# The skip path of a hybrid encoder layer moved into the attention stage, and the first softmax map left unscaled

## The chip, the cores and the metric

One NeuronCore of a Trainium2 chip runs the kernel. The metric is the device time of one execution in microseconds, the median of several runs. TensorE, VectorE (DVE), ScalarE (ACT), GpSimd (POOL) and SyncE (SP) each work through a queue of their own in order; transfers are issued by the queue of an engine and carried out by 16 DMA engines.

## What is computed

One encoder layer on x of 1024 tokens by 1024 channels, float32. x is normalised row by row (LayerNorm with ln_emb). One input projection of width 6688 feeds two groups that run side by side: a bidirectional state-space group (convolution, chunked scan in both directions, gated RMS norm) and a differential attention of 8 heads. Both outputs, 2 x 1024 channels, go through one output projection, and the result is added to the skip path and normalised. What matters for the change:

```
h = layer_norm(x, ln_emb_g, ln_emb_b)
probs = softmax(scores, axis=-1)
w = probs[:, :, 0] - lam * probs[:, :, 1]
o = einsum("bhqs,bshe->bqhe", w, v)
o = rms_norm(o, subln_g) * (1.0 - lam_init)
y_attn = o * silu(g)
mix = einsum("bse,ed->bsd", concat([y_ssm, y_attn]), w_out)
out = layer_norm(ALPHA * h + mix, ln_g, ln_b)
```

`rms_norm` divides by the square root of the mean square plus 1e-5. If a query's row of w is multiplied by the sum s0 of its first map's exponentials, o grows by s0, and the RMS norm gives the same result when 1e-5 is replaced by 1e-5 times s0 squared. That is what lets the first map stay unscaled.

## The kernel before

**Stages.** The kernel normalises x, transposes it and keeps it in SBUF as a high and a low part (`hh`, `hl`), so that three fast matmuls stand for one float32 product. The input projection runs as 52 blocks of 128 output channels (`fill`, L328), each with 48 matmuls of 128x512. Weights are loaded by SP (`wst`), their high part is cast by ScalarE (`whi`) and the low part subtracted by GpSimd (`wlo`). The state-space group uses TensorE up to about 430 us, the attention from there. The output projection (`project_out`, L1245) has 16 units of 48 matmuls: for each of 8 token blocks `tb` a part 0 (the state-space half) and a part 1 (the attention half). Part 0 can run while head 7 is still at work; part 1 needs all heads. The rows of w_out are cast and split as they come (`rows_out`, L1137: tiles `ws`, `oh`, `ol`, later `or`).

**What sets the order.** The work is written as lanes (Python generators), and a planner, `Loom` (L46), chooses which lane goes on next, from ranks and margins in `LANES` (L29) and from costs that it assumes for each operation (L175 to L213). TensorE's order is what the planner chose; the other engines' instructions are put in order by the framework's own scheduler from its estimates, and then each engine runs its queue strictly in that order. SP issues every transfer of this kernel (`dma`, L250). All engine calls go through one helper, so nearly all rows carry its line, L140; tiles tell them apart.

**Attention of one head.** `scores` (L981): for each of 8 query blocks two score maps of 128x1024 in PSUM (`sc`), VectorE subtracts the distance penalty and takes the row maximum (`p`, `nm`), ScalarE takes the exponential with its row sum `ls`. `combine` (L1016): VectorE takes reciprocals of both sums (`rs`), multiplies one by the negative lambda, GpSimd multiplies the first map by its reciprocal (L1028; in head 7 ScalarE does, L1026), and VectorE combines both maps. `values` (L1033): TensorE transposes the combined map, ScalarE and VectorE evict it as a high and a low part (`wh`, `wl`), and it is multiplied with v. `finish` (L1070), once for each half head of 512 queries: squares (`osq`, `osh`, `osl`), their sum over channels by TensorE, the RMS factor (`msq`, `rt`) and the gate; four stores to `yd` in DRAM. PSUM banks for all but the scores come from a ring of four (`bk`).

**Skip path.** `residuals` (L1189) starts when the memory of head 6 is given back, near 1000 us. For each token block and half row it loads x (`xr`, L1212), computes `nmr` on VectorE, normalises on ScalarE, multiplies by ALPHA times the gain (`g_e`) and adds ALPHA times the bias (`b_e`) on GpSimd. `project_out` adds the PSUM result of part 0 to `xr` on VectorE (L1280) and `norm_out` (L1221) does the last LayerNorm with `g_o`, `b_o`. Pieces of the token blocks 5 to 7 are loaded late, into tiles that the attention gives back.

**Other transfers that the change touches.** `z_block` (L466) stores SiLU(z) to DRAM (`zd<-zs`, 16 of 256 KB, L478). `proj_k` (L909) copies each half of the key tile to the other partitions (`kk<-kk`, 32 of 128 KB, L921).

Of the kernel before, what the change touches and what calls it, by code (L numbers as in the profile page):

```python
# [27 lines left out]

LANES = dict(weights=(0, 0.8), channels=(1, 1.2), steps=(2, 1.6), z_tail=(2, 0.8), conv=(3, 1), v_tail=(3, 0.4), states=(4.4, 0.8), diag=(4.125, 0.6), maps=(4.4, 0.6), gate=(4.375, 0.2), finish=(4.2, 2), scores=(4, 0.8), combine=(4.125, 0.6), values=(4.25, 0.4), fill=(9, 0.8), rows_out=(9, 0.2), y_out=(9, 3), residuals=(9, 2), project_out=(9, 2))  # L29

# [186 lines left out]
def hybrid_layer_kernel(  # L217
# [14 lines left out]
    AO = Engine(loom, nc.scalar, "ACT", _act_cost, pinned=True)  # L232
    SP = Engine(loom, nc.sync, "DMA", _dma_cost)
    x, out = x[0], out[0]
    w_in, w_out, conv_w = w_in[0], w_out[0], conv_w[0]
# [14 lines left out]
    def dma(dst, src):  # L250
        SP.dma_start(dst, src)

    def transpose(dst, src, n=128):
# [111 lines left out]
    acs_dr = [dr.tile([16, NCH, 128], F32, name=f"acs_d{d}") for d in range(2)]  # L365
    zd = [dr.tile([NCH, 128, 512], F32, name=f"zd{g}") for g in range(2)]


# [97 lines left out]
    def z_block(g, j, when=None):  # L466
        def evac(half, ps):
            zr = late["sq"].tile([128, 512], F32, name="zr", bufs=2)
            A.copy(zr, ps)

            def tail():
                pt = bank((128, 4, 128))
                yield (zr, pt)
                for i in range(4):
                    transpose(pt[:, i, :], zr[:, 128 * i:128 * i + 128])
                zs = late["sq"].tile([128, 4, 128], F32, name="zs", tag="zr", bufs=2)
                A.activation(zs, pt, AF.Silu)
                dma(zd[g][4 * half:4 * half + 4, :, 128 * j:128 * j + 128].rearrange("c p n -> p c n"), zs)  # L478
                G[g].z_done += 1
            loom.add(tail(), "z_tail")  # L480
        queue.append(Block(Z0 + 512 * g + 128 * j, evac, when))
# [397 lines left out]
    class Head:  # L879
        def __init__(self, h):  # L880
            self.pool = lambda: ep if h % 2 == 0 else att["op"]
            self.q, self.k, self.v, self.g = [], 0, 0, 0
            self.scored = self.summed = self.done = 0

# [24 lines left out]
    def proj_k(h):  # L909
        H = heads_[h]  # L910

        def evac(half, ps):
            if half == 0:
                H.kk = H.pool().tile([128, 2, S], F32R, name="kk")
                H.kl = H.pool().tile([128, S], F32R, name="kl")
            t = slice(512 * half, 512 * half + 512)
            for m in range(2):
                a, b = slice(64 * m, 64 * m + 64), slice(64 - 64 * m, 128 - 64 * m)
                A.copy(H.kk[a, m, t], ps[a])
                V.tensor_sub(H.kl[a, t], ps[a], H.kk[a, m, t].bitcast(F32))  # L920
                dma(H.kk[b, m, t].bitcast(F32), H.kk[a, m, t].bitcast(F32))  # L921
            H.k += 1
        queue.append(Block(K0 + 128 * h, evac, free_since(h, "scored", 8)))
# [57 lines left out]
    def scores():  # L981

        for h, H in enumerate(heads_):
            m_h = 2.0 ** -(h + 1)
            for tb in range(8):
                yield lambda: len(H.q) > tb // 4 and H.k == 2
                yield lambda: count["s"] - count["t"] < 2
                nm = ap.tile([128, 2], F32, name="nm", bufs=2)
                ls = ap.tile([128, 2], F32, name="ls", bufs=2)
                q = H.q[tb // 4]  # L990
# [12 lines left out]
                for m in range(2):  # L1003
# [5 lines left out]
                    A.activation(p, p, AF.Exp, scale=-1.0, bias=nm[:, m:m + 1],  # L1009
                                 accum_out=ls[:, m:m + 1])  # L1010
                    pm_.append(p)
# [4 lines left out]
    def combine():  # L1016

        for _ in range(64):
            yield lambda: bool(raw_maps)
            H, tb, (p0, p1), ls = raw_maps.pop(0)  # L1020
            yield (p1, ls)
            rs = ap.tile([128, 2], F32, name="rs", bufs=2)
            V.reciprocal(rs, ls)
            V.tensor_mul(rs[:, 1:2], rs[:, 1:2], neg_lam)
            if H is heads_[7]:
                A.activation(p0, p0, AF.Copy, scale=rs[:, 0:1])  # L1026
            else:
                P.tensor_scalar(p0, p0, rs[:, 0:1], 1.0, op0=ALU.mult, op1=ALU.mult)  # L1028
            yield p0
            V.scalar_tensor_tensor(p0, p1, rs[:, 1:2], p0, op0=ALU.mult, op1=ALU.add)  # L1030
            maps_.append((H, tb, p0))

    def values():  # L1033
# [36 lines left out]
    def finish(H, o, half):  # L1070

        h = heads_.index(H)
        osq = ap.tile([128, 512], F32, name="osq")
        A.activation(osq, o, AF.Square)
# [28 lines left out]
    queue[-2].pair = queue[-1].last = True  # L1103
    for lane in (scores, combine, values):
        loom.add(lane())
# [78 lines left out]

    res = {}
    used = set()
    halves = [slice(0, 512), slice(512, 1024)]

    def residuals():  # L1189

        yield lambda: "pool" in res
        for n, src in (("g", ln_emb_g), ("b", ln_emb_b)):
            res[n] = res["pool"].tile([128, D], F32, name=n + "_e")
            dma(res[n], src.partition_broadcast(128))
            A.activation(res[n], res[n], AF.Copy, scale=ALPHA)
        late = [("zr", 2), ("zr", 2), ("o", 2), ("o", 2), ("osq", 1), ("msq", 1)]
        for tb in range(8):
# [5 lines left out]
            xr = []  # L1203
            nmr = ap.tile([128, 1], F32, name="nmr", bufs=2)
            V.scalar_tensor_tensor(nmr, mv[tb][:, 0:1], -1.0, rstd[tb], op0=ALU.mult, op1=ALU.mult)
# [11 lines left out]
        for n, src in (("g", ln_g[0]), ("b", ln_b[0])):  # L1217
            res[n + "o"] = res["pool"].tile([128, D], F32, name=n + "_o", tag=n + "_e")
            dma(res[n + "o"], src.partition_broadcast(128))

# [97 lines left out]
```

## Time and profile before

| | |
|---|---|
| median of 3 runs | 1236.02 us (1235.99 to 1239.23) |
| the profiled execution's own time | 1237.79 us |
| its span | 1236.1 us |
| mean granted TensorE clock, share of full speed | 0.989 |
| instructions | 16491 |

The profile is of one execution. Busy time counts an engine's instructions, not its waits. A wait is put down to the event that came last before the instruction could start. "Granted clock" is TensorE's, as a share of 2.4 GHz; its lower level is 1.2 GHz.

### The profile page before, as it was taken

The numbers are of one execution on the slowest core, as the hardware profiler recorded it, in microseconds if no ns is written. First come the engines' busy times: TensorE is split into PE (matmuls) and PEld (weight loads), VectorE is DVE, ScalarE is ACT, GpSimd is POOL, SyncE is SP. The second block draws the span as 40 slices with busy tenths as digits, with TensorE's granted clock in tenths as the row PEclk, the third lists the DMA queues.
The fourth block names the chain that finished last, engine by engine and source line by source line (L and its number), as shares of the span: only waits on it lengthen the run. The fifth ranks groups of instructions, "written<-read, shape, count | busy, mean of one in ns | idle before, by whom it ended". The sixth has DMA issues, their size and how long they took to land. (4 is left out here: it accounts for less than half of the span.)

```text
span 1236.1 us, 16491 instructions
## 1 busy us (share of the span) xinstructions
PE 1177.5 (95%) x5881; PEld 923.5 (75%) x5881; DVE 903.5 (73%) x1303; ACT 702.8 (57%) x1281; POOL 472.6 (38%) x404
## 2 busy tenths in 40 slices
PE   5999999899989999999999999999999998999997
PEld 3777667788667777778787777878778776778885
DVE  6686876767875568788788887887878889952334
ACT  4557478734468456565655657556655686641221
POOL 7412564322753223323232333233232429541354
PEclk9999999999999999999999999999999999989999
DMA  6113236522345521011111121121111262233221
GB/s 198 34 32 116 81 110 173 181 65 53 99 118 149 151 63 43 26 46 50 26 48 39 43 53 26 34 52 36 43 36 42 86 225 83 74 103 114 77 86 60
DMA packets 107592, 98.04 MB, mean 79 GB/s; under 512 B 9364, under 2 KB 79349, under 8 KB 107509
## 3 DMA queue, kind: packets, MB, share of 16 engines
q1 hardware_dynamic: 107509, 96.98, 27.4%
q8 instruction: 46, 0.75, 0.3%
q14 instruction: 37, 0.30, 0.1%
HBM read 75.85 MB, written 16.91 MB: 75 GB/s over the span
## 5 line engine op out<-in xcount | busy, mean ns | idle before, releaser
L140 PE MATMUL bk<-hh,whi 128*128 128x512 f32 x832 | 353.8, 425 | 1.3 <-DVE yt L140 0.7
L140 PE MATMUL bk<-hl,whi 128*128 128x512 f32 x832 | 328.1, 394 | 3.3 <-POOL hl L140 3.0
L140 PE MATMUL bk<-hh,wlo 128*128 128x512 f32 x832 | 328.9, 395 | 0.0
L140 POOL TENSOR_TENSOR wlo<-wst,whi 128x512 fp32r<-128x512 f32 x104 | 160.4, 1546 | 145.1 <-ACT whi L140 129.0
L140 ACT ACTIVATE p<-p,nm 128x1024 f32<-128x1024 f32 x128 | 146.8, 1148 | 121.3 <-DVE nm L140 120.6
L140 POOL TENSOR_SCALAR p<-p,rs 128x1024 f32<-128x1024 f32 x56 | 64.5, 1152 | 350.1 <-DVE rs L140 300.4
L140 PEld LDWEIGHTS bk<-hh,whi 128*128 128x128 f32 x832 | 158.3, 190 | 33.8 <-issue 5.7
L140 PEld LDWEIGHTS bk<-hh,wlo 128*128 128x128 f32 x832 | 157.2, 189 | 35.3
L140 PEld LDWEIGHTS bk<-hl,whi 128*128 128x128 f32 x832 | 158.3, 190 | 33.2 <-POOL hl L140 5.5
L140 DVE CUSTOM_DVE_ANT_0 p<-sc,dist 128x1024 f32<-128x1024 f32 x128 | 151.3, 1217 | 11.9 <-PE sc L140 11.2
L140 DVE SCALAR_TENSOR_TENSOR p<-p,rs,p 128x1024 f32<-128x1024 f32 x64 | 127.8, 1997 | 22.6 <-POOL p L140 18.0
L140 DVE TENSOR_TENSOR wl<-bk,wh 128x512 fp32r<-128x512 f32 x128 | 86.9, 683 | 16.1 <-ACT wh L140 14.2
L140 ACT CAST wh<-bk 128x512 fp32r<-128x512 f32 x128 | 74.1, 579 | 43.1 <-PE bk L140 42.4
L140 ACT CAST whi<-wst 128x512 fp32r<-128x512 f32 x104 | 64.0, 621 | 44.4 <-PE bk L140 37.5
L140 PE MATMUL bk<-ident,p 128*128 128x128 f32 x512 | 79.9, 279 | 4.7 <-DVE wl L140 3.0
L140 PEld LDWEIGHTS bk<-ident,p 128*128 128x128 f32 x512 | 61.9, 142 | 29.5 <-DVE wl L140 6.5
L140 ACT ACT_TABLE_LOAD x46 | 59.0, 1283 | 27.9 <-DVE t L140 17.2
L140 PE MATMUL bk<-wh,vh 128*128 128x256 f32 x256 | 74.6, 291 | 0.0
L140 PE MATMUL bk<-wl,vh 128*128 128x256 f32 x256 | 72.2, 282 | 0.9 <-DVE wl L140 0.9
L140 PE MATMUL sc<-kk,q 128*128 128x512 f32 x256 | 72.4, 394 | 0.0
L140 PE MATMUL bk<-wh,vl 128*128 128x256 f32 x256 | 72.0, 281 | 0.0
L140 PEld LDWEIGHTS bk<-xt,t 128*128 128x128 f32 x256 | 44.9, 189 | 24.3 <-issue 15.8
(217 smaller groups left out, 2168.3 us busy)
## 6 DMA issues: line engine op xcount, KB each, us to landing
wst<-in_w_in_dram SPq DMA_DIRECT2D x104, 256.0 KB, 3.0
t<-acs_d SPq DMA_DIRECT2D x64, 256.0 KB, 3.4
ws<-in_w_out_dram SPq DMA_DIRECT2D x32, 256.0 KB, 3.1
ys<-yd SPq DMA_DIRECT2D x32, 256.0 KB, 3.1
xb<-in_x_dram SPq DMA_DIRECT2D x8, 512.0 KB, 6.3
zd<-zs SPq DMA_DIRECT2D x16, 256.0 KB, 3.0
gz<-zd SPq DMA_DIRECT2D x16, 256.0 KB, 3.1
yd<-ys SPq DMA_DIRECT2D x16, 256.0 KB, 2.5
```

Source lines behind the costliest of these rows:

```text
L140: r = f(*args, **kw)
```

## The change

1. The skip path is computed in a new lane, `skip_rows`, during the attention: 16 pieces of 128x512, one after every third query block, each loaded, normalised (ScalarE), multiplied and added to (GpSimd) and stored to DRAM (`xr_dram`). `residuals` only loads the finished pieces. `g_o` and `b_o` are loaded before head 7.
2. The first map is not scaled. The second map's factor becomes -lam times s0 / s1, with one map-wide operation in `combine` instead of two. Every four query blocks ScalarE squares s0 with the factor sqrt(1e-5) (`e2`) and sends the 512 values through DRAM (`ed`); `finish` loads them as a row over all partitions (`er`) and adds them where 1e-5 was added.
3. The RMS factor's refinement takes one VectorE operation less.
4. ScalarE's queue issues the stores of zs, the copies of kk and those of ed.
5. The memory set aside for another kind of DMA is cut to 1024 bytes, which makes room for the new tiles.

The new lane has rank 9, margin 2. The diff, cut:

```diff
+    AD = Engine(loom, nc.scalar, "DMA", _dma_cost)
+    def dma_act(dst, src):
+        AD.dma_start(dst, src)
+    xr_dram = [dr.tile([128, D], F32, name=f"xrd{b}") for b in range(NCH)]
-                dma(zd[g][4 * half:4 * half + 4, :, 128 * j:128 * j + 128].rearrange("c p n -> p c n"), zs)
+                dma_act(zd[g][4 * half:4 * half + 4, :, 128 * j:128 * j + 128].rearrange("c p n -> p c n"), zs)
-                dma(H.kk[b, m, t].bitcast(F32), H.kk[a, m, t].bitcast(F32))
+                dma_act(H.kk[b, m, t].bitcast(F32), H.kk[a, m, t].bitcast(F32))
-                ls = ap.tile([128, 2], F32, name="ls", bufs=2)
+                if tb % 4 == 0:
+                    ls = ap.tile([128, 4, 2], F32, name="ls", bufs=2)
 ...
-            rs = ap.tile([128, 2], F32, name="rs", bufs=2)
-            V.reciprocal(rs, ls)
-            V.tensor_mul(rs[:, 1:2], rs[:, 1:2], neg_lam)
-            if H is heads_[7]:
-                A.activation(p0, p0, AF.Copy, scale=rs[:, 0:1])
-            else:
-                P.tensor_scalar(p0, p0, rs[:, 0:1], 1.0, op0=ALU.mult, op1=ALU.mult)
-            yield p0
-            V.scalar_tensor_tensor(p0, p1, rs[:, 1:2], p0, op0=ALU.mult, op1=ALU.add)
+            rs = ap.tile([128, 1], F32, name="rs", bufs=2)
+            V.reciprocal(rs, ls[:, tb % 4, 1:2])
+            V.scalar_tensor_tensor(rs, rs, ls[:, tb % 4, 0:1], neg_lam, op0=ALU.mult, op1=ALU.mult)
+            V.scalar_tensor_tensor(p0, p1, rs, p0, op0=ALU.mult, op1=ALU.add)
             maps_.append((H, tb, p0))
+            if tb % 4 == 3:
+                e2 = ap.tile([128, 4], F32, name="e2", bufs=2)
+                A.activation(e2, ls[:, :, 0], AF.Square, scale=math.sqrt(EPS))
+                ed = dr.tile([4, 128], F32, name="ed", bufs=2)
+                    dma_act(ed.rearrange("t p -> p t"), e2)
+                H.ed.append(ed)
 ...
+        er = ap.tile([128, 512], F32, name="er")
+        dma(er, H.ed[half].rearrange("t p -> (t p)").partition_broadcast(128))
-        V.tensor_scalar(ms, pms, 1.0 / 128, EPS, op0=ALU.mult, op1=ALU.add)
+        V.scalar_tensor_tensor(ms, pms, 1.0 / 128, er, op0=ALU.mult, op1=ALU.add)
 ...
-        V.tensor_mul(ms, ms, rt)
-        V.tensor_scalar(ms, ms, -0.5, 1.5, op0=ALU.mult, op1=ALU.add)
+        V.scalar_tensor_tensor(ms, ms, -0.5, rt, op0=ALU.mult, op1=ALU.mult)
+        V.scalar_tensor_tensor(rt, ms, 1.5, rt, op0=ALU.add, op1=ALU.mult)
-        V.tensor_mul(rt, rt, ms)
 ...
+    def skip_rows():
+        for n, src in (("g", ln_emb_g), ("b", ln_emb_b)):
+            resid[n] = ap.tile([128, D], F32, name=n + "_e")
+            dma(resid[n], src.partition_broadcast(128))
+        yield lambda: count["s"] > 1
+        for n in "gb":
+            A.activation(resid[n], resid[n], AF.Copy, scale=ALPHA)
+        left = []
+        def store():
+            dst, t = left.pop(0)
+            dma(dst, t)
+        for i in range(16):
+            tb, t = i // 2, slice(512 * (i % 2), 512 * (i % 2) + 512)
+            yield lambda: count["s"] >= 3 * i + 3
+            if len(left) > 1:
+                store()
+            xe = ap.tile([128, 512], F32, name="xe", bufs=2)
+            dma(xe, x[128 * tb:128 * tb + 128, t])
+            nmr = ap.tile([128, 1], F32, name="nmr", bufs=2)
+            V.scalar_tensor_tensor(nmr, mv[tb][:, 0:1], -1.0, rstd[tb], op0=ALU.mult, op1=ALU.mult)
+            A.activation(xe, xe, AF.Identity, scale=rstd[tb], bias=nmr)
+            P.tensor_mul(xe, xe, resid["g"][:, t])
+            P.tensor_add(xe, xe, resid["b"][:, t])
+            left.append((xr_dram[tb][:, t], xe))
+        yield lambda: count["s"] >= 54
+        while left:
+            store()
+        for n, src in (("g", ln_g[0]), ("b", ln_b[0])):
+            res[n + "o"] = ap.tile([128, D], F32, name=n + "_o", tag=n + "_e")
+            dma(res[n + "o"], src.partition_broadcast(128))
 ...
-                dma(xr[n], x[128 * tb:128 * tb + 128, t])
-                A.activation(xr[n], xr[n], AF.Identity, scale=rstd[tb], bias=nmr)
-                P.tensor_mul(xr[n], xr[n], res["g"][:, t])
-                P.tensor_add(xr[n], xr[n], res["b"][:, t])
+                dma(xr[n], xr_dram[tb][:, t])
 ...
```

`count["s"]` is the number of query blocks whose scores are done, 64 in all.

## Rows read from the trace of the kernel before

**Rows 1.** The page's first part: busy time, share of the span, instructions, by engine.

```profile
PE 1177.5 (95%) x5881; PEld 923.5 (75%) x5881; DVE 903.5 (73%) x1303; ACT 702.8 (57%) x1281; POOL 472.6 (38%) x404
```

**Rows 2.** Busy time by stretch: length, PE, PEld, DVE, ACT, POOL, granted clock, DMA share, GB/s.

```profile
430.00:980.00 550.00, 548.11 (x2943) 432.70 (x2941) 440.90 (x659) 334.19 (x581) 168.59 (x124) 1.00 0.17 43
980.00:1100.00 120.00, 108.67 (x553) 85.98 (x552) 98.42 (x139) 83.34 (x138) 59.95 (x41) 0.96 0.39 123
1100.00:1228.30 128.30, 128.28 (x554) 103.76 (x552) 48.43 (x83) 28.93 (x45) 55.54 (x45) 1.00 0.28 88
```

**Rows 3.** TensorE's timeline from 975 to 1100: start, us, work, [idle before, releaser].

```profile
1021.41 0.39 PE L140 MATMUL bk<-wl,vh 128*128 128x256 f32 x1 [0.91 <-DVE wl L140]
...
1029.96 0.51 PE L140 MATMUL bk<-oh,oyh 128*128 128x512 f32 x1 [3.98 <-DVE xr L140]
...
1047.76 1.09 PE L140 MATMUL bk<-oh,oyh 128*128 128x512 f32 x2 [1.02 <-DVE wl L140]
...
1086.29 1.11 PE L140 MATMUL bk<-ident,p 128*128 128x128 f32 x4 [2.87 <-DVE wl L140]
```

**Rows 4.** Busy time by stretch, columns as in rows 2, after the two long gaps.

```profile
1029.96:1034.65 4.69, 4.69 (x15) 3.77 (x16) 4.66 (x6) 4.69 (x9) 4.69 (x4) 0.64 0.18 59
...
1086.29:1092.78 6.49, 6.49 (x20) 5.34 (x21) 4.41 (x7) 2.31 (x4) 1.72 (x2) 0.54 0.37 105
```

**Rows 5.** The chain that ended last, around the gap at 1083: start, us, what.

```profile
1078.59 4.24 DMA xr<-in_x_dram
...
1082.93 0.04 ACT xr L140
...
1083.65 0.61 ACT or L140
...
1085.63 0.61 DVE wl L140
```

**Rows 6.** Groups of VectorE from 1016 to 1062: count, busy us, mean ns, idle before.

```profile
L140 DVE TENSOR_TENSOR oyl<-ys,oyh 128x512 fp32r<-128x512 f32 x5 | 8.1, 1636 | 0.0
L140 DVE SCALAR_TENSOR_TENSOR p<-p,rs,p 128x1024 f32<-128x1024 f32 x4 | 7.4, 1862 | 0.7 <-ACT p L140 0.6
...
L140 DVE SCALAR_TENSOR_TENSOR nmr<-mv,rstd 128x1 f32<-128x1 f32 x6 | 5.3, 889 | 1.2 <-ACT xr L140 1.1
```

**Rows 7.** VectorE's timeline, the same two operations with GpSimd idle.

```profile
995.39 1.28 DVE L140 SCALAR_TENSOR_TENSOR p<-p,rs,p 128x1024 f32<-128x1024 f32 x1 [0.36 <-ACT p L140]
...
1008.76 0.68 DVE L140 TENSOR_TENSOR oyl<-ys,oyh 128x512 fp32r<-128x512 f32 x1
```

**Rows 8.** Busy time of the tile xr alone: length, DVE, ACT, POOL, clock, DMA.

```profile
980.00:1100.00 120.00, 5.34 (x8) 10.03 (x13) 39.36 (x26) 0.96 0.39 123
```

**Rows 9.** Groups from 430 to 1000, columns as in rows 6.

```profile
L140 DVE SCALAR_TENSOR_TENSOR p<-p,rs,p 128x1024 f32<-128x1024 f32 x57 | 115.6, 2028 | 18.4 <-POOL p L140 18.0 <-ACT p L140 0.4
...
L140 POOL TENSOR_SCALAR p<-p,rs 128x1024 f32<-128x1024 f32 x56 | 64.5, 1152 | 350.1 <-DVE rs L140 300.4 <-PE bk L140 49.7
```

**Rows 10.** Issues on SP by tile: count, ns least/median/most, first and last start.

```profile
L140 SPq DMA_DIRECT2D zd<-zs x16: 359/370/508, 122.2 to 392.2; - x16
...
L140 SPq DMA_DIRECT2D kk<-kk x32: 461/467/1127, 409.6 to 967.7; - x32
```

**Rows 11.** Waits: who for whom, us in total, times, longest.

```profile
ACT xr L140 <- DMA xr<-in_x_dram: 7.6, 3, 5.8
...
PE bk L140 <- DVE t L140: 3.5, 4, 1.3
...
SPq L140 <- ACT kk L140: 62.4, 16, 7.9
...
SPq L140 <- ACT zs L140: 27.8, 10, 7.2
```

**Rows 12.** Transfers: count, KB each, median us from issue to landing.

```profile
zd<-zs SPq DMA_DIRECT2D x16, 256.0 KB, 3.0
...
xr<-in_x_dram SPq DMA_DIRECT2D x16, 256.0 KB, 5.4
```

More of the change, by code (lines that the diff above doesn't have):

```diff
@@ L27 @@
 ALPHA = 2.0 ** 0.25
-LANES = dict(weights=(0, 0.8), channels=(1, 1.2), steps=(2, 1.6), z_tail=(2, 0.8), conv=(3, 1), v_tail=(3, 0.4), states=(4.4, 0.8), diag=(4.125, 0.6), maps=(4.4, 0.6), gate=(4.375, 0.2), finish=(4.2, 2), scores=(4, 0.8), combine=(4.125, 0.6), values=(4.25, 0.4), fill=(9, 0.8), rows_out=(9, 0.2), y_out=(9, 3), residuals=(9, 2), project_out=(9, 2))
+LANES = dict(weights=(0, 0.8), channels=(1, 1.2), steps=(2, 1.6), z_tail=(2, 0.8), conv=(3, 1), v_tail=(3, 0.4), states=(4.4, 0.8), diag=(4.125, 0.6), maps=(4.4, 0.6), gate=(4.375, 0.2), finish=(4.2, 2), skip_rows=(9, 2), scores=(4, 0.8), combine=(4.125, 0.6), values=(4.25, 0.4), fill=(9, 0.8), rows_out=(9, 0.2), y_out=(9, 3), residuals=(9, 2), project_out=(9, 2))
 def col_bcast(ap, n):
@@ L882, in __init__ @@
             self.q, self.k, self.v, self.g = [], 0, 0, 0
+            self.ed = []
             self.scored = self.summed = self.done = 0
@@ L1009, in scores @@
                     A.activation(p, p, AF.Exp, scale=-1.0, bias=nm[:, m:m + 1],
-                                 accum_out=ls[:, m:m + 1])
+                                 accum_out=ls[:, tb % 4, m:m + 1])
                     pm_.append(p)
@@ L1021, in combine @@
             yield (p1, ls)
-            rs = ap.tile([128, 2], F32, name="rs", bufs=2)
-            V.reciprocal(rs, ls)
-            V.tensor_mul(rs[:, 1:2], rs[:, 1:2], neg_lam)
-            if H is heads_[7]:
-                A.activation(p0, p0, AF.Copy, scale=rs[:, 0:1])
-            else:
-                P.tensor_scalar(p0, p0, rs[:, 0:1], 1.0, op0=ALU.mult, op1=ALU.mult)
-            yield p0
-            V.scalar_tensor_tensor(p0, p1, rs[:, 1:2], p0, op0=ALU.mult, op1=ALU.add)
-            maps_.append((H, tb, p0))
+            rs = ap.tile([128, 1], F32, name="rs", bufs=2)
+            V.reciprocal(rs, ls[:, tb % 4, 1:2])
+            V.scalar_tensor_tensor(rs, rs, ls[:, tb % 4, 0:1], neg_lam, op0=ALU.mult, op1=ALU.mult)
+            V.scalar_tensor_tensor(p0, p1, rs, p0, op0=ALU.mult, op1=ALU.add)
+            maps_.append((H, tb, p0))
+            if tb % 4 == 3:
+                e2 = ap.tile([128, 4], F32, name="e2", bufs=2)
+                A.activation(e2, ls[:, :, 0], AF.Square, scale=math.sqrt(EPS))
+                ed = dr.tile([4, 128], F32, name="ed", bufs=2)
+                with nc.allow_non_contiguous_dma(reason="512 words"):
+                    dma_act(ed.rearrange("t p -> p t"), e2)
+                H.ed.append(ed)
     def values():
@@ L1103, in hybrid_layer_kernel @@
     queue[-2].pair = queue[-1].last = True
-    for lane in (scores, combine, values):
+    resid = {}
+    def skip_rows():
[28 more added lines that the diff above has]
+            dma(res[n + "o"], src.partition_broadcast(128))
+    res = {}
+    for lane in (scores, combine, values, skip_rows):
         loom.add(lane())
@@ L1183, in y_out @@
             ahead[tb, part] = parts
-    res = {}
     used = set()
@@ L1191, in residuals @@
         yield lambda: "pool" in res
[L1192 to L1195, printed above, removed]
         late = [("zr", 2), ("zr", 2), ("o", 2), ("o", 2), ("osq", 1), ("msq", 1)]
@@ L1203, in residuals @@
             xr = []
-            nmr = ap.tile([128, 1], F32, name="nmr", bufs=2)
-            V.scalar_tensor_tensor(nmr, mv[tb][:, 0:1], -1.0, rstd[tb], op0=ALU.mult, op1=ALU.mult)
             for n, t in enumerate(halves):
@@ L1211, in residuals @@
                     xr.append(ap.tile([128, 512], F32, name="xr", tag=tag, bufs=bufs))
-                dma(xr[n], x[128 * tb:128 * tb + 128, t])
-                A.activation(xr[n], xr[n], AF.Identity, scale=rstd[tb], bias=nmr)
-                P.tensor_mul(xr[n], xr[n], res["g"][:, t])
-                P.tensor_add(xr[n], xr[n], res["b"][:, t])
+                dma(xr[n], xr_dram[tb][:, t])
             res[tb] = xr
-        for n, src in (("g", ln_g[0]), ("b", ln_b[0])):
-            res[n + "o"] = res["pool"].tile([128, D], F32, name=n + "_o", tag=n + "_e")
-            dma(res[n + "o"], src.partition_broadcast(128))
     def norm_out(tb, xr, po, final):
@@ L1304 @@
     from concourse.bass_utils import run_bass_kernel_spmd as _run
-    nc = _bacc.Bacc("TRN2", target_bir_lowering=False, num_devices=1)
+    nc = _bacc.Bacc("TRN2", target_bir_lowering=False, num_devices=1,
+                     dynamic_dma_scratch_size=1024)
     arrays, args = {}, []
```

## The prediction

> **What bounds the kernel now.** I read the page's busy shares first [rows 1]: TensorE is busy 95% of the span, VectorE 73%, ScalarE 57%. An average hides stages with different limits, so next came busy time by stretch [rows 2]. The reader should see three stages there. From 430 to 980 us, heads 0 to 6, TensorE is busy 548.11 of 550 us: whatever VectorE, ScalarE or GpSimd save there is worth almost nothing. From 980 to 1100, where head 7 runs beside the output projection, 11.3 of 120 us are idle. From 1100 to 1228.3 TensorE is full again. So the change is priced in the middle stage, and in 430 to 980 only for harm.
>
> The waits of TensorE's own timeline [rows 3] give the idle time: 0.91, 3.98, 1.02 and 2.87 us, together 8.8 us (the other 2.5 us are shorter waits, left alone here). After the two long ones the granted clock falls [rows 4]: mean 0.64 over 4.69 us and 0.54 over 6.49 us, towards 1.2 GHz from 2.4. Work lost: 0.36 x 4.69 = 1.7 us and 0.46 x 6.49 = 3.0 us. Gaps and their aftermath cost **13.5 us**; the row of 1100 to 1228.3 has no such loss.
>
> **Why those gaps exist.** The chain of waits names the path through the last of them [rows 5]: an xr load took 4.24 us, ScalarE stood until it landed, its next w_out cast and evictions came after, VectorE's subtraction after those, and TensorE lacked a free PSUM bank. The 3.98 us gap ends on VectorE's addition of xr to the product: the bank was held until the skip path was ready. Both are the in-line skip computation. VectorE is also slowed while GpSimd works: between 1016 and 1062 us, 5 oyl subtractions took 1.636 us each, 4 combinations of p 1.862 and 6 one-column nmr products 0.889 [rows 6]. Outside, an oyl took 0.68 and a combination 1.28 [rows 7]. Excess: 5 x 0.96 + 4 x 0.58 + 5.3 for nmr, which leaves this stage whole, = 12.4 us in a stretch of 46. GpSimd spends 39.36 us on xr's 26 products and sums in this stage, ScalarE 10.03 us on 13 normalisations [rows 8].
>
> **The change part by part.**
> *Skip path moved.* The stage loses those 39.36 us of GpSimd, 10.03 of ScalarE, the nmr products, and the scaling of g_e and b_e; an xr is now a plain load from DRAM, which only VectorE's addition waits for. Two parameter loads leave SP's queue here too. The 3.98 us gap goes with its slow clock: 5.7 us. The 2.87 us gap goes with its own, 5.9 us; next late there is the split of w_out, for which I leave 0.5. The 1.02 us gap stands behind VectorE's backlog and goes. The 0.91 us gap follows two ol subtractions of GpSimd that stay: I count half, 0.45. **Gain 5.7 + 5.4 + 1.0 + 0.45 = 12.5 us.** The three late pieces of xr after 1100 us lie under full TensorE: nothing.
>
> *First map unscaled.* In heads 0 to 6, 56 GpSimd products of 1.152 us (64.5 us) go [rows 9], and the combination starts that much sooner; in head 7 ScalarE did the scaling and is relieved. The cover in 430 to 980 is TensorE's own queue, so 0; head 7's share is inside the gaps above. The shorter RMS chain (one 128x512 VectorE operation fewer in each of 16 finishes) is covered the same way: 0. If the cover went, VectorE would be next, busy 441 of 550 [rows 2].
>
> *What that stage receives.* Sixteen pieces of skip path: a load, a normalisation (10.03 / 13 = 0.77 us on ScalarE), two GpSimd operations (39.36 / 26 = 1.51 us) and a store each. GpSimd thus gets 48 us back for 64.5. The issue on SP: xe has two buffers, and a load waits until the store two pieces earlier has landed, 3.0 us for such a store; the load itself took 5.4 at its median in the crowded stage [rows 12]. On SP the weight, er and y transfers queue behind that wait; TensorE waits for none of them within a few us. ScalarE's normalisation waits for the load, and the attention's exponentials and evictions queue behind it. Bounds for TensorE: below 0; above 16 x 5.8 us, the longest wait of ScalarE for an xr load [rows 11], 93 us. I take what such loads did before, 7.6 us of waiting in all over 16 loads [rows 11], of which TensorE pays a fifth: **1.5 us**. The low end is nearer because of [rows 9]: 57 combinations took 2.028 us instead of 1.28, 43 us of delay, and TensorE paid at most 1.9 us of idle time in the stage.
>
> *Issues moved from SP to ScalarE.* An issue took 0.370 us for zs and 0.467 for kk [rows 10]. In the attention 32 of kk and 16 of ed come to 48 x 0.467 = 22 us on ScalarE, busy 334 of 550. Each also waits for ScalarE's own result, with the next eviction behind it. Bounds: 0 to 22 us; I take **0.5**, by the same tolerance. SP stood 62.4 us for kk and 27.8 for zs [rows 11], but nothing of TensorE's was late behind it in the attention, so the relief there is 0. In the earlier stage the t loads stand behind zs, and TensorE waited 3.5 us for DVE t [rows 11]; the 16 zs issues cost ScalarE 5.9 us. So between a gain of 3.5 and a loss of 5.9: 0.
>
> *Epsilon row.* Sixteen squares of 128x4 on ScalarE, each between 0 and the 0.77 us of a 128x512; 512 words stored per half head, no row for that shape. Its latency is hidden behind the transposes and values of that half, and er's load behind the square and the sum over partitions; if it landed late, only head 7's last y would be late, and the other half of the output projection is there to run before it. 0.
>
> **Sum.** 12.5 - 1.5 - 0.5 = 10.5 us. The profiled execution took 1237.79 us for a span of 1236.1, and stands 1.77 over the median of 1236.02. 1236.02 - 10.5 = **1225.5 us**.
>
> **A rule that speaks against it.** VectorE operations on two SBUF tensors stretch while GpSimd runs: 1.636 us against 0.68 [rows 6, 7]. The Trainium skill, "Advanced Engine Details and Errata", section Miscellaneous Facts, GPSIMD Details, says that the Pool engine shares a read and a write interface with VectorE and conflicts with operations that have two SBUF inputs. By that rule, with which these rows agree, the stretch is not removed but moved into the attention. As a mechanism: 32 moved GpSimd operations x 0.96 us = 31 us more on VectorE. The sum holds that at 0, since GpSimd loses more than it gets; the rival below takes the other side.
>
> **The rivals.**
> *Something else fills the gaps.* The w_out splits and head 7's own chain are late by themselves, so only the 5.7 us around the xr addition is won: 1236.0 - 5.7 + 2 = 1232.3. For it: GpSimd's ol and ScalarE's or casts stand in the same chain [rows 5]. Against: each was queued behind xr work.
> *The stretch moves along.* TensorE pays a quarter of the 31 us: 1225.5 + 7.8 = 1233.3. Against: the 43 us of delay that cost it nothing.
> *ScalarE stands in line: slower.* If the normalisations reach ScalarE before their loads land, each stops every exponential and eviction. With 7.6 / 3 = 2.5 us for each of 16 pieces, 40 us, of which TensorE pays half: 1236.0 - 12.5 + 0.5 + 20 = 1244. It decides from (12.5 - 0.5) / 16 = 0.75 us of TensorE time per piece. For it: the 5.8 us wait. Against: 13 of 16 such loads caused no wait, and DMA is at 0.17 in this stage against 0.39 [rows 2].
> *More is won.* The 3.5 us behind t in the earlier stage and the 2.5 us of shorter waits go as well: 1225.5 - 6.0, about 1220.
>
> **How the numbers follow.** About 0.3%, 3.7 us, is what a measurement of this kernel can tell from no change: faster is under 1232.3, slower over 1239.7. Forecast (1222 to 1230) 0.52; more is won 0.14; something else fills the gaps 0.18, on the border, half faster and half same; the stretch moves along 0.07, 0.02 of it faster; ScalarE in line 0.09, slower. Faster 0.52 + 0.14 + 0.09 + 0.02 = 0.77, same 0.14, slower 0.09. The range runs from 1217, below the case in which more is won, to 1236, above the two partial cases; outside are the slower case and some 0.08 more.
>
> **What would show it.** In the changed profile: no TensorE wait of over 1 us between 1000 and 1100 that ends on DVE xr or follows an ACT xr; oyl near 0.7 us there; granted clock 1.00 from 980 to the last matmul; 430 to 980 still over 99% busy. Wrong would be: waits of ScalarE for an xe load over 20 us in total with TensorE idle beside them; gaps of the same size now ended by or, wl or a ws load; or a loss before 430 us behind zs.

## The result and the profile after

The changed kernel takes **1278.28 us** (median of 4 runs, 1274.73 to 1280.25) against 1236.01 for the kernel before in the same session (1234.51 to 1239.23): ratio 1.0335, 95% interval 1.0305 to 1.0366. The forecast was 1225.5, 1217 to 1236; the kernel became 42 us slower. The profiled execution took 1278.51 us for a span of 1276.8.

First the busy shares of the page and the busy time of TensorE by stretch (length, busy, granted clock, DMA share, GB/s) of the changed kernel.

```profile
PE 1181.3 (93%) x5881; PEld 929.4 (73%) x5881; DVE 863.1 (68%) x1295; ACT 699.6 (55%) x1289; POOL 400.2 (31%) x348
```

```profile
430.00:600.00 170.00, 143.15 (x708) 0.92 0.38 105
600.00:1000.00 400.00, 399.77 (x2184) 1.00 0.24 48
1000.00:1150.00 150.00, 129.70 (x650) 0.93 0.37 104
```

The first and the last of these stretches in the kernel before:

```profile
430.00:600.00 170.00, 169.56 (x911) 1.00 0.17 46
...
1000.00:1150.00 150.00, 140.83 (x670) 0.97 0.37 116
```

VectorE and GpSimd have less to do than before [rows 1], and that bought nothing. The loss sits in two stretches. From 430 to 600 us TensorE was full before (169.56 of 170); now 26.9 us are idle and the clock is at 0.92. From 1000 to 1150 20.3 us are idle, where it was 9.2 (140.83 busy) before. TensorE's gaps over 3 us from 430 us on (start, us, work, [idle before, releaser]):

```profile
490.93 1.09 PE L140 MATMUL bk<-ident,p 128*128 128x128 f32 x4 [12.38 <-DVE kl L140]
500.60 0.92 PE L140 MATMUL sc<-kk,q 128*128 128x512 f32 x2 [4.33 <-DVE nm L140]
517.24 0.65 PE L140 MATMUL bk<-ident,vc 128*128 128x128 f32 x4 [4.12 <-ACT vc L140]
532.69 1.11 PE L140 MATMUL bk<-ident,vc 128*128 128x128 f32 x4 [3.01 <-ACT vc L140]
...
1050.50 1.22 PE L140 MATMUL sc<-kk,q 128*128 128x512 f32 x2 [7.07 <-DVE nm L140]
1140.48 1.39 PE L140 MATMUL bk<-oh,oyh 128*128 128x512 f32 x2 [4.54 <-DVE wl L140]
```

VectorE and ScalarE release them, but the waits of ScalarE lead on to transfers (us in total, times, longest):

```profile
ACT xe L140 <- DMA xe<-in_x_dram: 33.2, 10, 11.8
...
ACT oh L140 <- DMA ws<-in_w_out_dram: 18.5, 3, 10.7
ACT or L140 <- DMA ws<-in_w_out_dram: 16.1, 6, 7.1
```

In the first stretch ScalarE stands for loads of the skip pieces. Their tile shows why there are so many at once (instruction, count, ns least/median/most, first and last start):

```profile
L140 SPq DMA_DIRECT2D xe<-in_x_dram x16: 327/384/497, 436.7 to 524.6; - x16
L140 ACT ACTIVATE xe<-xe,nmr,rstd x16: 797/816/827, 442.6 to 528.1; 128x512 f32<-128x512 f32 x16
```

All sixteen pieces run back to back in the first 100 us of the attention, not one after every third query block. The longest of these waits, 11.8 us, is for two loads that SP issued at 473.5, 0.7 us after the first store of ed. They take 13.1 us to land (view from 472.5 to 486.5):

```profile
xe<-in_x_dram SPq DMA_DIRECT2D x2, 256.0 KB, 13.1
```

In the second stretch ScalarE stands for a load of w_out. Its timeline and SP's (start, us, engine, operation), and then the transfers from 1032 to 1048 us (GB/s in 40 slices of 0.4 us, packets by queue, median us from issue to landing):

```profile
1033.59 0.36 ACTq L140 DMA_DIRECT2D ed<-e  x1
...
1046.79 1.29 ACT L140 CAST oh<-ws 128x512 fp32r<-128x512 f32 x2 [10.65 <-DMA ws<-in_w_out_dram]
```

```profile
1034.08 1.48 SPq L140 DMA_DIRECT2D ws<-in_w_out_dram  x3
1045.46 0.33 SPq L140 DMA_DIRECT2D er<-ed  x1
```

```profile
GB/s 46 0 0 0 0 0 5 0 0 0 0 0 15 15 0 56 20 5 15 15 20 10 20 20 5 10 15 5 15 15 36 67 41 20 271 338 405 425 307 215
...
q10 hardware_dynamic: 528, 0.00, 1.6%
...
ws<-in_w_out_dram SPq DMA_DIRECT2D x3, 256.0 KB, 12.8
```

ScalarE issues ed at 1033.59. Three loads of w_out, issued 0.5 us later, land after 12.8 us (the median of all 32 in this kernel is 3.9), and for some 11 us all 16 DMA engines together move less than 70 GB/s, mostly 20 or less. My first reading missed this: I saw that SP waits 180.9 us in all for ed before it issues er, and took that standing for the cause.

### The profile page after: what moved, and what is told of

It reads as the page before. It is cut to its first block, busy times and chain, and to the rows that moved or that the text cites. A ratio compares the mean times of both kernels' runs of the same rounds, so it can differ in the third digit from the quotient of the medians.

```text
span 1276.8 us, 16387 instructions
## 1 busy us (share of the span) xinstructions
PE 1181.3 (93%) x5881; PEld 929.4 (73%) x5881; DVE 863.1 (68%) x1295; ACT 699.6 (55%) x1289; POOL 400.2 (31%) x348
## 4 chain that ended last, share of the span: by engine, by line
PE 56%; DVE 13%; issue 9%; DMA 8%; ACT 6%; POOL 4%; SPq 1%; ACTq 0%; DVEq 0%; POOLq 0%
PE bk L140 44%; PE sc L140 9%; DMA ws<-in_w_out_dram 3%; PE sb L140 3%; DMA xe<-in_x_dram 3%; POOL xe L140 2%; DVE yt L140 2%; DVE p L140 2%; ACT p L140 2%; DVE t L140 2%; DVE xc L140 1%; SPq L140 1%; DVE xw L140 1%; DVE sm L140 1%; DVE c_ch L140 1%
## 5 line engine op out<-in xcount | busy, mean ns | idle before, releaser
L140 POOL TENSOR_TENSOR wlo<-wst,whi 128x512 fp32r<-128x512 f32 x104 | 147.8, 1425 | 329.4 <-ACT whi L140 300.1
L140 PE MATMUL bk<-ident,p 128*128 128x128 f32 x512 | 80.4, 281 | 18.3 <-DVE kl L140 12.4
L140 POOL TENSOR_TENSOR o<-o,gate 128x512 f32<-128x512 f32 x16 | 31.1, 1942 | 190.7 <-ACT osq L140 190.7
L140 DVE SCALAR_TENSOR_TENSOR p<-p,rs,p 128x1024 f32<-128x1024 f32 x64 | 84.8, 1325 | 2.2
L140 PEld LDWEIGHTS bk<-xt,t 128*128 128x128 f32 x256 | 45.4, 191 | 30.8 <-issue 20.3
```

Of the source, the lines that this page charges most:

```text
L140: r = f(*args, **kw)
```

## The experiments

All are the changed kernel with one thing undone or altered, unless told otherwise. The last three columns are TensorE's idle us by stretch (length less busy time; the stretches are the same for all, though a slower kernel comes to its output stage later). Ratios are to the kernel before in the same session. The kernel before had medians from 1232.99 to 1236.01 us in the six sessions, so differences between runs of different sessions are taken from the ratios below, times 1234 us (0.001 is 1.2 us).

| kernel | median us | ratio (95%) | 430-600 | 600-1000 | 1000-1150 |
|---|---|---|---|---|---|
| before | 1236.01 | | 0.4 | 3.6 | 9.2 |
| changed | 1278.28 | 1.0335 (1.0305-1.0366) | 26.9 | 0.2 | 20.3 |
| 1 skip path alone | 1251.97 | 1.0155 (1.0135-1.0175) | 14.8 | 1.5 | 7.9 |
| 2 unscaled map and row alone | 1248.99 | 1.0130 (1.0108-1.0152) | 2.4 | 2.9 | 20.8 |
| 3 no trip | 1248.03 | 1.0123 (1.0104-1.0142) | 17.7 | 0.0 | 7.0 |
| 4 zs, kk on SP | 1272.43 | 1.0324 (1.0293-1.0354) | 26.3 | 0.2 | 17.9 |
| 5 pieces held | 1284.20 | 1.0399 (1.0371-1.0427) | 3.1 | 5.4 | 46.3 |
| 6 rows of 16 bytes, order by queries left out | 1252.48 | 1.0138 (1.0115-1.0162) | 17.7 | 0.2 | 8.8 |
| 7 epsilon on diagonals | 1278.46 | 1.0365 (1.0329-1.0401) | 16.9 | 16.2 | 12.4 |
| 8 = 5 + 7 | 1276.25 | 1.0328 (1.0287-1.0369) | 2.7 | 28.7 | 11.7 |
| 9 pieces spread | 1242.54 | 1.0087 (1.0067-1.0107) | 3.7 | 3.6 | 12.3 |
| 10 rows of 16 bytes | 1249.28 | 1.0139 (1.0123-1.0156) | 17.8 | 0.2 | 8.2 |
| 11 = 9 + 10 | 1232.21 | 0.9989 (0.9974-1.0004) | 3.7 | 2.8 | 5.0 |
| 12 spread, no trip | 1226.30 | 0.9950 (0.9932-0.9968) | 3.3 | 2.9 | 4.3 |
| 13 er behind o | 1278.62 | 1.0358 (1.0337-1.0379) | 24.6 | 0.3 | 21.0 |
| 14 = 9 + 13 | 1247.37 | 1.0096 (1.0080-1.0113) | 3.9 | 2.7 | 16.8 |
| 15 = 9 + 10 + 13 | 1229.75 | 0.9958 (0.9942-0.9975) | 3.2 | 2.5 | 4.7 |
| 16 = 12 + 512 words, unread | 1246.04 | 1.0100 (1.0075-1.0126) | 3.9 | 2.8 | 16.7 |
| 17 = 12 + rows of 16, unread | 1230.95 | 0.9978 (0.9964-0.9992) | 4.6 | 0.7 | 6.8 |

### Which part: runs 1 to 4

Run 1 leaves the maps, the constant epsilon and the issues as in the kernel before:

```diff
-            V.scalar_tensor_tensor(rs, rs, ls[:, tb % 4, 0:1], neg_lam, op0=ALU.mult, op1=ALU.mult)
+            V.tensor_mul(rs[:, 1:2], rs[:, 1:2], neg_lam)
...
-        V.scalar_tensor_tensor(ms, pms, 1.0 / 128, er, op0=ALU.mult, op1=ALU.add)
+        V.tensor_scalar(ms, pms, 1.0 / 128, EPS, op0=ALU.mult, op1=ALU.add)
```

> Only the skip path's move, added to the kernel before: maps scaled by GpSimd, epsilon a constant, zs and kk issued by SP. It tells the skip pieces from the epsilon row. Theory T (the row's trip through DRAM holds SP's queue, and all loads behind it are late): without the trip nothing is late, 1222 to 1232 us. Theory B (the sixteen skip pieces, bunched at the start of the attention, hold ScalarE, VectorE and SP): the loss between 430 and 600 us stays, 27 us idle and 11 at the slow clock, and the one after 1000 goes: 1255 to 1268. Both together (the 12.4 us gap is the trip's, the shorter ones are the pieces'): 1238 to 1252.

Run 2 is the kernel before with the changed lines of `scores`, `combine` and `finish`:

```diff
+                    dma_act(ed.rearrange("t p -> p t"), e2)
...
+        dma(er, H.ed[half].rearrange("t p -> (t p)").partition_broadcast(128))
```

> Only the unscaled map and the epsilon row, added to the kernel before: ed is stored by ScalarE's queue and er loaded by SP's as in the changed kernel; the skip path stays in the output stage, zs and kk stay on SP. Theory T: the loss after 1000 us appears beside the one that the skip path causes there already, and a gap near 480 us too: 1250 to 1275. Theory B: the row costs nothing, and the shorter chain of the maps may win a little: 1232 to 1237. Both: 1243 to 1258, with a loss in the output stage alone.

Run 3:

```diff
-                    dma_act(ed.rearrange("t p -> p t"), e2)
...
-        V.scalar_tensor_tensor(ms, pms, 1.0 / 128, er, op0=ALU.mult, op1=ALU.add)
+        V.tensor_scalar(ms, pms, 1.0 / 128, EPS, op0=ALU.mult, op1=ALU.add)
```

> The changed kernel without the row: ed, its square and er are left out, and the mean square gets the constant epsilon (this leaves out the scaling of epsilon by the square of each query's sum). Theory T: 1222 to 1232. Theory B: 1255 to 1268. Both: 1238 to 1252, with the 12.4 us gap at 478 and the 7.1 us gap at 1043 gone, the ScalarE waits for xe loads still there, 15 to 25 us in all.

Run 4:

```diff
-                dma_act(H.kk[b, m, t].bitcast(F32), H.kk[a, m, t].bitcast(F32))
+                dma(H.kk[b, m, t].bitcast(F32), H.kk[a, m, t].bitcast(F32))
```

> The changed kernel with zs and kk issued by SP again, ed still by ScalarE. If the 48 issues on ScalarE are the cost, about 22 us of it comes back: 1250 to 1262. If not (theories T and B, and both), 1275 to 1290, since SP's queue gets the waits for kk on top of those for ed and xe.

"Both" holds in runs 1 to 3. The skip path by itself loses time from 430 to 600, the row by itself from 1000 to 1150. In run 3 a gap of 3.9 us stands where the one of 12.4 was, and ScalarE still stands 23.5 us for xe loads, ten times, 4.2 us at most. The issues that ScalarE took over are not the cause: run 4's median is 2.6 us under the range for that, but its ratio and the changed kernel's cover each other.

### Holding the pieces, shortening the store: runs 5 to 8

Run 5 pins the pieces' instructions behind what their engine was given before. It also gives each load a lead of one block of scores over its normalisation, and runs 8, 9, 11, 12 and 14 to 17 have both edits:

```diff
-            dma(xe, x[128 * tb:128 * tb + 128, t])
+            SO.dma_start(xe, x[128 * tb:128 * tb + 128, t])
+            yield lambda: count["s"] >= 3 * i + 4
...
-            A.activation(xe, xe, AF.Identity, scale=rstd[tb], bias=nmr)
+            AO.activation(xe, xe, AF.Identity, scale=rstd[tb], bias=nmr)
```

> The changed kernel with the sixteen skip pieces held to their places among the scores: each load, normalisation, product, sum and store is kept behind what its engine was given before it, and a piece's normalisation comes one block of scores after its load. The row's trip stays. Both theories together: the pieces' part goes, some 24 us by the run with the trip left out, and the trip's part stays: 1246 to 1260, the gap near 1043 still there. If the pieces did harm only because their loads stood behind ed (the trip alone is the cause): the waits for ed hit other loads instead and the time stays at 1270 to 1282. If ScalarE's waits for xe only move along the attention: 1262 to 1275, with over 15 us of ScalarE waiting for xe loads.

None of the three. The first stretch was full again, but the pieces had gone to the worst place, the output stage:

```profile
L140 ACT ACTIVATE xe<-xe,nmr,rstd x16: 798/813/819, 997.0 to 1124.6; 128x512 f32<-128x512 f32 x16
```

So the lane's code is written at the output stage. That its last rank, 9, gives it no turn earlier is what run 9 tries.

Run 6:

```diff
-                ed = dr.tile([4, 128], F32, name="ed", bufs=2)
-                    dma_act(ed.rearrange("t p -> p t"), e2)
+                ed = dr.tile([128, 4], F32, name="ed", bufs=2)
+                dma_act(ed, e2)
```

> The changed kernel with ed stored as it lies in SBUF, 128 rows of 16 bytes in place of 512 words of 4 bytes, and er read from that (this leaves out the order by queries: each query gets the epsilon of another one of its 512). The same bytes, the same place in every queue, a quarter of the pieces. Theory scatter (the store is late because it is 512 words): ed lands in under 4 us in place of 8.6, SP's waits for ed fall from 181 to 80 to 110 us, and half of the trip's 30 us comes back: 1258 to 1268. Theory place (any trip that SP waits for there costs this): ed's landing falls or not, SP's waits stay over 140 us, 1272 to 1282.

Scatter, and by more than I gave it: the same bytes from the same queue at the same place, and by the ratios 24 of the trip's 26 us come back (1.0335, 1.0138, and 1.0123 without the trip). ScalarE's longest wait for an xe load falls from 11.8 to 4.6 us.

Run 7:

```diff
-        dma(er, H.ed[half].rearrange("t p -> (t p)").partition_broadcast(128))
+            V.scalar_tensor_tensor(osq[:, t], ident, H.ed[half][:, j:j + 1], osq[:, t], op0=ALU.mult, op1=ALU.add)
```

> The changed kernel with the same epsilon by queries but no DRAM: 128 times the row's values are put on the diagonals of the four 128x128 blocks of osq by four VectorE operations with the identity, so that the sum over partitions that is there anyway adds them. 64 VectorE operations of 128x128 more, ed and er gone. If the trip is the cost and not the work on the row: as the run that leaves the row out, 1245 to 1251. If VectorE's extra work shows: 1252 to 1258.

A miss. ScalarE waits 0.7 us at most for w_out before an oh cast, and 20.6 us in all for the xe loads, whose pieces are where they were. But the 64 operations of 0.34 us stand in `finish` between ScalarE's square and its cast:

```profile
L140 DVE SCALAR_TENSOR_TENSOR osq<-ident,e,osq x64: 335/340/1451, 505.3 to 1154.4; 128x128 f32<-128x128 f32 x64
...
  DVE osq L140: 32.6, 14
```

ScalarE waits for them 14 times, 32.6 us in all, and TensorE, whose order is fixed, is idle 16.2 us from 600 to 1000, where the changed kernel loses 0.2. Run 8 is runs 5 and 7 in one. It misses all of its ranges and has the loss of the 64 operations still, 28.7 us idle from 600 to 1000:

> Both remedies at once: the skip pieces held to their places, and the epsilon on the diagonals. All of the computation is there. Both theories together: neither loss is left and the gain of the output stage shows: 1222 to 1230, below the kernel before. If the skip path costs as much spread out as bunched: 1240 to 1250. If the output stage's gain was never there: 1232 to 1238.

### Pieces in their places: runs 9 to 12

Run 9, beside the pins of run 5:

```diff
-skip_rows=(9, 2)
+skip_rows=(3.9, 2)
```

> The run with the pieces held to their places put them at 997 to 1125 us: their lane has the last rank, 9, gets no turn while TensorE is the bound, and so its code is written late, at the output stage; left unpinned, the framework moves it to the start of the attention instead. Here the lane gets rank 3.9, before the scores, and the pieces stay held: two in each head. The row's trip stays as it is. If bunching is the pieces' whole cost: 430 to 600 us is full again and the trip's cost after 1000 stays, 1246 to 1260. If the pieces cost as much wherever they stand: 1270 to 1285.

Run 10 is run 6 with each query's own epsilon, by a strided view:

```diff
-        V.scalar_tensor_tensor(ms, pms, 1.0 / 128, er, op0=ALU.mult, op1=ALU.add)
+        V.scalar_tensor_tensor(ms.rearrange("p (t q) -> p t q", **tq), pms.rearrange("p (t q) -> p t q", **tq), 1.0 / 128,
+                               er.rearrange("p (q t) -> p t q", **tq), op0=ALU.mult, op1=ALU.add)
```

> The changed kernel with ed stored as 128 rows of 16 bytes and er read back through a strided view inside VectorE's operation, so that each query gets its own epsilon: the whole computation is there. As the run with 16-byte rows: 1249 to 1255, ed landing in some 2 to 3 us. If the strided read of er slows VectorE so that it shows: 1256 to 1264.

Run 11 has both edits, run 12 the spread pieces with run 3's constant epsilon.

> Both remedies: the lane at rank 3.9 with the pieces held, and ed in rows of 16 bytes with the strided view. The whole computation is there. If bunching and the scattered store are the two causes: 1222 to 1232, at or below the forecast made for the change itself, and below the kernel before. If the pieces cost as much spread out as bunched: 1246 to 1256.

> The lane at rank 3.9 with the pieces held, and a constant epsilon without ed and er (this leaves out the scaling of epsilon by the square of each query's sum). It is the bound for the run with both remedies: 1221 to 1229 if the short trip still costs a little there, equal to it if it costs nothing. If the gain forecast for the output stage (12.5 us) isn't there: 1232 to 1238.

Runs 10 and 12 came out where bunching and the scattered store are the two causes. Run 11 is 0.2 us over its range and cannot be told from the kernel before, where it was to be below. Run 9 is below its range: by the ratios, bunching costs 31 us where the store is there. The pieces of run 11 lie over the whole attention, and ScalarE waits for none of their loads:

```profile
L140 SPq DMA_DIRECT2D xe<-in_x_dram x16: 423/468/656, 438.1 to 910.0; - x16
L140 ACT ACTIVATE xe<-xe,nmr,rstd x16: 797/802/807, 468.4 to 924.4; 128x512 f32<-128x512 f32 x16
...
  ACT xe L140: 137.1, 16
```

(The last line is GpSimd's wait for ScalarE, the only one on this tile.) "Spread" in these runs means rank, pins and the lead of the loads together: the first load is now issued 30 us before its normalisation. Which of the three takes the waits away was not tried apart. The strided read of er makes its operation 1.056 us in place of 0.682 (run 10, medians of 16), and no time is lost by it that can be seen.

### The queue or the words: runs 13 to 17

SP waits for ed in the changed kernel, and the 512 words of ed are under way at the same moment. Runs 13 and 14 take the wait away and leave the words:

```diff
-        dma(er, H.ed[half].rearrange("t p -> (t p)").partition_broadcast(128))
+        EO.dma_start(er, H.ed[half].rearrange("t p -> (t p)").partition_broadcast(128))
```

`EO` is ScalarE's queue, held in order, so er stands behind the copy of o; by the trace of run 9 the square of o, right behind it, starts 13 to 26 us after ed.

> The changed kernel with one issue moved: er's load goes from SP's queue to ScalarE's, held behind the copy of o, 13 us or more after the store of ed; the 512 words stay, and so do the bunched pieces. Theory standing (SP's queue standing for ed is the trip's cost): no engine waits for ed any more, and the time is that of the run without the trip, 1245 to 1252. Theory words (the 512 words cost by themselves): 1262 to 1280.

> The same move with the pieces spread (rank 3.9, held). The whole computation is there, and ed is still 512 words. Theory standing: 1225 to 1231, as the run without the trip, and below the kernel before. Theory words: 1236 to 1243, as the run with the spread pieces and the trip on SP.

> Pieces spread, er behind the copy of o on ScalarE's queue, and ed in rows of 16 bytes with the strided view. Theory standing: within 2 us of the run with the 512 words, 1225 to 1231. Theory words: below it by 6 us or more, 1225 to 1232 against 1236 to 1243.

Theory standing, which was mine, falls: no queue waits for ed any more, and both times stay: by the ratios run 13 cannot be told from the changed kernel, nor run 14 from run 9 (1.0096, 1.0087), though run 14's median is 4 us over both of its ranges. In run 14 ScalarE still waits for w_out right behind ed, at 1014 us:

```profile
1000.50 0.36 ACTq L140 DMA_DIRECT2D ed<-e  x1
...
1014.11 1.26 ACT L140 CAST oh<-ws 128x512 fp32r<-128x512 f32 x2 [11.75 <-DMA ws<-in_w_out_dram]
```

Runs 16 and 17 put only the square and the store into the kernel of run 12, read by nobody, run 16 as 512 words and run 17 as 128 rows. Run 16's edit against run 12:

```diff
+                A.activation(e2, ls[:, :, 0], AF.Square, scale=math.sqrt(EPS))
+                    dma_act(ed.rearrange("t p -> p t"), e2)
```

> The kernel with spread pieces and a constant epsilon (1226), plus the square and the store of ed as 512 words, which nothing reads (the scaling of epsilon is left out as there). Theory words: nearly all of the trip's cost is back, 1238 to 1248, with loads of w_out or y that land 11 to 13 us after their issue beside an ed store, and DMA rates under 60 GB/s for some 10 us there. Theory reader (the load of er and the wait for it are needed for the cost): 1225 to 1230.

> The same with ed stored as 128 rows of 16 bytes, which nothing reads. Theory words: 1225 to 1230, as without any store. If the number of small pieces counts in proportion: a quarter of the cost of the 512 words, 1229 to 1232.

Run 16, its transfers from 1000 to 1012 us:

```profile
GB/s 0 0 0 0 0 7 0 0 0 0 0 0 0 7 7 7 7 48 27 14 14 7 20 20 20 14 20 14 7 14 7 7 14 14 7 7 14 7 14 75
DMA packets 592, 0.13 MB, mean 11 GB/s; under 512 B 529, under 2 KB 529, under 8 KB 592
...
q10 hardware_dynamic: 528, 0.00, 2.1%
...
ws<-in_w_out_dram SPq DMA_DIRECT2D x3, 256.0 KB, 13.0
...
ed<-e ACTq DMA_DIRECT2D x1, 2.0 KB, 9.8
```

Run 17, from 1002.5 to 1014.5, with the same 2 KB in 128 rows:

```profile
DMA packets 1009, 1.59 MB, mean 133 GB/s; under 512 B 240, under 2 KB 240, under 8 KB 1008
...
q10 hardware_dynamic: 144, 0.00, 0.6%
...
ws<-in_w_out_dram SPq DMA_DIRECT2D x5, 256.0 KB, 4.7
...
ed<-e ACTq DMA_DIRECT2D x1, 2.0 KB, 1.4
```

By the ratios the store alone, unread, costs 18.5 us (0.9950 to 1.0100): in the 12 us around it, 11 GB/s move in place of 133. TensorE has the changed kernel's gap of 7.07 us again, here as

```profile
1017.71 1.22 PE L140 MATMUL sc<-kk,q 128*128 128x512 f32 x2 [7.31 <-DVE nm L140]
```

In rows of 16 bytes the store costs 3.5 us (0.9978; the two intervals just overlap), near the quarter that the count of pieces would give. Whether the number of the pieces or their size of 4 bytes counts was not tried apart. The two causes with their crossings, as ratios to the kernel before:

| pieces of the skip path | 512 words | rows of 16 bytes | no row |
|---|---|---|---|
| bunched at 430 to 530 | changed: 1.0335, run 13: 1.0358 | run 10: 1.0139 | run 3: 1.0123 |
| spread over the attention | runs 9, 14: 1.0087, 1.0096 | runs 11, 15: 0.9989, 0.9958 | run 12: 0.9950 |

Run 15 computes everything that the changed kernel does and is faster than both kernels: 0.9958 (0.9942 to 0.9975) of the kernel before. Run 11 cannot be told from the kernel before.

## Why the prediction was wrong

**The epsilon row, taken at 0: one of the two steps that failed.** I asked only whether er would be late for its own reader. For that the step was right: VectorE waits for er nowhere in the changed kernel's trace, and moving er gained nothing (runs 13, 14). What failed is that I priced 512 words as latency of one transfer, and not as something that holds up the loads beside it, though I wrote that there was no row for that shape: a cost without a row needed an upper bound, and got none. Measured by the ratios: 18.5 us alone (run 16 over run 12), 26 beside the bunched pieces (the changed kernel over run 3).

The Trainium skill, "DMA: Bandwidth & Descriptors", section Rules for kernel authors, says that a strided last dimension becomes one descriptor per element and should be rearranged to be contiguous. The traces agree: 528 packets on ScalarE's queue with the words, 144 with the rows of 16 bytes, that is 512 and 128 and 16 more each. The same page, section Queues, rings and completion order, says that each DMA engine takes turns between the queues packet by packet. The trace of run 16 does not show such turns as the cost. All 528 packets of ed are on record between 1001 and 1002 us (first view); from 1002 to 1011.5 none of them is left, and the loads crawl all the same (second view):

```profile
q10 hardware_dynamic: 528, 0.00, 25.4%
```

```profile
DMA packets 51, 0.10 MB, mean 11 GB/s; under 512 B 0, under 2 KB 0, under 8 KB 51
...
q1 hardware_dynamic: 51, 0.10, 23.5%
```

These 51 packets of 2 KB took 0.70 us each (23.5% of 16 engines' 9.5 us); the 864 on that queue in the window of run 17 took 0.09. What holds them until ed has landed stays open.

**The skip pieces, taken at 1.5 us: the other step.** The price per piece was argued for pieces one after every third query block. That assumption fell: the lane has the last rank and its code comes late, and the framework, free to move it, put all pieces at the start of the attention. My own front pages said that VectorE's, ScalarE's and GpSimd's order is the framework's, and I did not apply it. Measured by the ratios: run 3 less run 12, 1.0123 - 0.9950, is 21 us, 1.3 per piece, above the 0.75 from which I had written that the rival decides. So the rival "ScalarE stands in line" was the mechanism (23.5 us of such waits in run 3; the changed kernel's 33.2 are the first of the signs of being wrong that I had named). That its price of 20 us was near is luck in part: it had 40 us of waits of which TensorE pays half. Its chance of 0.09 was a mistake.

The misreading can be found in the trace of the kernel before. There the pieces were no less bunched: twelve loads of xr were issued from 994 to 1015 us and twelve normalisations ran from 1020 to 1044. But each of these loads had a lead of 20 us or more, and none was waited for. The last four, into tiles that the attention gives back, were issued 3 to 5 us ahead, and three of them are the three waits. First a line of SP and one of ScalarE in the kernel before, then two from the changed kernel:

```profile
1012.74 2.32 SPq L140 DMA_DIRECT2D xr<-in_x_dram  x5
1042.24 1.52 ACT L140 ACTIVATE xr<-xr,nmr,rstd 128x512 f32<-128x512 f32 x2 [1.56 <-DVE nmr L140]
```

```profile
493.20 1.94 SPq L140 DMA_DIRECT2D xe<-in_x_dram  x2
495.89 0.81 ACT L140 ACTIVATE xe<-xe,nmr,rstd 128x512 f32<-128x512 f32 x1 [4.17 <-DMA xe<-in_x_dram]
```

With two buffers for xe and the pieces back to back, no load can be issued far ahead. So the 7.6 us of waiting belonged to four loads, not to sixteen; taken so, sixteen pieces come to 30 us. Spread and with their lead, the pieces do what the forecast said: run 12 has no such wait.

The two steps together make the miss: from run 12 to the changed kernel (0.9950 to 1.0335) it is 48 us, more than the 18.5 and 21 by themselves. One reason is in the trace: the longest wait for a piece, 11.8 us, is beside a store of ed, and without the row the longest is 4.2 (run 3).

**The issues on ScalarE, 0.5 us, and the z stores, 0.** Not contradicted, to some 4 us: run 4's ratio cannot be told from the changed kernel's, and the first scores of the attention start at 430.9 us in the changed kernel and at 430.3 before.

**The gain of 12.5 us: right in kind, about half in size.** The stretched VectorE operations of the output stage are gone. These are its groups from 1000 to 1100 us in the changed kernel (count, busy us, mean ns, idle before):

```profile
L140 DVE SCALAR_TENSOR_TENSOR p<-p,rs,p 128x1024 f32<-128x1024 f32 x8 | 10.8, 1350 | 0.2
...
L140 DVE TENSOR_TENSOR oyl<-ys,oyh 128x512 fp32r<-128x512 f32 x9 | 6.2, 685 | 0.1
```

[rows 6] had 1862 and 1636 ns. No wait for an xr load is left, and the gap behind the addition of xr, 3.98 us in [rows 3], is 0.83 in run 12. But run 12, free of both faults, is at 0.9950, some 6 us below the kernel before, where the sum had 10.5. What is late instead is the eviction of o by ScalarE; the gaps over 1 us of run 12 from 960 to 1240 us:

```profile
998.56 0.66 PE L140 MATMUL bk<-ident,p 128*128 128x128 f32 x4 [2.39 <-ACT o L140]
...
1015.39 0.66 PE L140 MATMUL bk<-ident,p 128*128 128x128 f32 x4 [1.50 <-ACT o L140]
1017.60 0.67 PE L140 MATMUL bk<-osh,ones_r 128*128 128x512 f32 x1 [1.55 <-DVE wl L140]
```

So of the gain's terms the gap behind xr came, and the others were partly replaced, as the rival "something else fills the gaps" had it: its 1232.3 is 3.7 us below 1236.0, the forecast was 10.5 below, and run 12 lies between.

**"The stretch moves along."** It did not reach TensorE at the rival's price of 7.8 us. Run 12 is the test, since its pieces lie between 468 and 926 us: TensorE is idle 2.9 us from 600 to 1000, 3.6 in the kernel before, and 0.2 in the changed kernel, whose pieces all ran earlier.

## What to carry to other kernels

Before a small transfer is called hidden, count its contiguous runs, not its bytes, and ask which other loads are under way while it runs: 512 words of 4 bytes held up the loads beside them for some 10 us, and where the next operation of a full engine waited for one, that was the price. Before waits are carried over from one stage to another, compare how long before its use each load was issued there and will be issued here. And where a scheduler may move code, "after every third block" in the source is no place: read from the order of the queues, or hold it there, where the work will run.

## What was not expected of the hardware

A store of 2 KB in 512 words takes 9.4 to 11.2 us to land (run 16, 16 of them), in 128 rows of 16 bytes 2.2 at the median (run 17). Before such a store has landed, loads of 256 KB on another queue are late: the slowest load of w_out took 9.1 to 13.0 us in the changed kernel and runs 2, 4, 9, 13, 14 and 16, and 5.8 to 6.1 in runs 3, 12 and 17; the median of run 12 is 2.9. ScalarE's longest wait for w_out before an oh cast tells the two kinds of kernel apart: 10.7 to 11.7 us in the changed kernel and runs 2, 4, 9, 13, 14 and 16, which have the words, and 3.1 to 3.9 in the kernel before and in runs 1, 3, 6, 10, 11, 12, 15 and 17, which don't. (Run 5, whose pieces fill this stage, has 5.5 there, and 13.3 before an or cast; runs 7 and 8 have 0.8 at most, and 2.8 before an or cast.) GpSimd's first product of a skip piece took 2050 ns at the mean with the pieces spread (run 11) and 1344 bunched (changed kernel), where VectorE often stood for ScalarE; that VectorE is the reason was not tried.
